# A two-layer decoder trunk in split fp32: low parts of the weights made by ScalarE and accumulating transfers instead of subtractions

## The chip, the cores and the metric

The kernel runs on one core of a Trainium2 chip. A core has five engines with queues of their own: TensorE (PE in the rows; its weight loads are PEld), VectorE (DVE), ScalarE (ACT), GpSimd (POOL) and SyncE (SP, which here only issues loads and stores), and 16 DMA engines that all queues share. The metric is the device time of one execution in microseconds; lower is better.

## The reference, cut to what matters

```python
h = jnp.concatenate([meta, x], axis=1)                     # 16 + 512 tokens, 1024 channels
for i in range(2):
    if i == 0:
        h = h + fox_conformer_mixer(rms_norm(h, ...), w_in, ..., w_out)
    else:
        h = h + multiscale_pool_mixer(rms_norm(h, ...), pool_w, pool_b, pool_scale)
    h = h + conv_glu_ffn(rms_norm(h, ...), w_up[i], conv_w[i], conv_b[i], w_down[i])
return rms_norm(h, final_norm)[:, 16:]

def fox_conformer_mixer(h, ...):
    q, k, v, f_logit, glu = split(h @ w_in)                # 8 heads of 64, 2 x 512 gated channels
    attn = softmax attention over q, k, v with forgetting (cumulated log sigmoid of f_logit)
    u = silu(layer_norm(causal_depthwise_conv(a * sigmoid(g), width 31)))
    return concatenate([attn, u]) @ w_out
def conv_glu_ffn(h, ...):
    u = causal_depthwise_conv(h @ w_up, width 3)           # 2 x 2816 channels
    gate, val = split(u); return (silu(gate) * val) @ w_down
```

All is computed in float32. The pooling mixer takes means over the last 2, 4, 8 or 16 tokens, less the token itself, and multiplies by one 256 x 256 matrix for each quarter of the channels.

## The kernel before

Channels lie on the partitions, the 528 tokens on the free axis. A float32 product is made from rounded parts: each activation x is split as xH + xL and each weight w as wH + wL, and of the four products xH wH, xL wH and xH wL are summed in PSUM (`product`, line 199; every matmul is issued by `mm`, line 197, and carries that line). A weight tile is 128 x 128; with two halves of 264 tokens it takes 6 matmuls.

The 1296 weight tiles come in the order in which TensorE uses them, as 162 chunks of 8 tiles (128 x 1024 float32, 512 KB each): 0 to 27 the mixer, 28 to 93 the first MLP, 94 and 95 the pooling, 96 to 161 the second MLP. `prepare(c)` (line 170) loads one raw chunk through SyncE's queue (line 173), makes wH by a rounding copy on ScalarE (line 223) or, for the 20 chunks of `VECTOR_CHUNKS`, on VectorE (line 224), and makes wL = raw - wH by a subtraction (line 178) on GpSimd for the 29 chunks of `POOL_CHUNKS`, else on VectorE. raw, wH and wL come from a pool of three buffers each; once the MLPs have begun, every fourth chunk takes its tiles from a further pool, `more`, which makes four. `ahead` (line 181) has two chunks prepared beyond the one in use.

Other places that are spoken of: `done_a` and `done_g` (lines 464 and 471) scale the gated projections, line 494 is a tap of the width-31 convolution on VectorE and line 498 one on GpSimd; lines 463 to 720 are the attention, with maxima (659, 663) and low parts of the probabilities (717). `scaled` (line 256) makes xH on ScalarE (258) and xL on VectorE (259). In the pooling, lines 1009 to 1036 scale by the norm, take window sums and add the residual. MLP tiles leave PSUM at line 952 and pass the width-3 convolution at 919 and 922. The norm's chain is line 277 to 283.

The framework orders each engine's instructions by a simulated time. Exceptions are blocks in which an order is written out by hand: the mixer (TensorE), the pooling (TensorE and VectorE) and the end (TensorE). Each engine's queue is served in order.

Of the kernel before, what the change touches and what calls it, by code (L numbers as in the profile page):

```python
# [15 lines left out]
P = 128  # L16
# [36 lines left out]
# output projection in two passes: (tile of the output, tiles of the contraction)  # L53
OUT_ORDER = [(m, (0, 1, 2)) for m in range(8)] + [(m, (4, 5, 6, 7, 3)) for m in range(8)]
# first tile of the output projection whose halves take PSUM from both pools
OUT_WIDE = 3
OUT_JOINT = 1
# tiles of the convolution branch split by VectorE alone
SPLIT_V = (0, 3)
POOL_CHUNKS = (6, 7, 8, 10, 13, 14, 15, 16, 17, 18, 19, 20, 21, 22, 23, 24, 25, 28, 31, 34, 97, 98, 100, 101, 102, 104, 105, 106, 107)  # L60
# what the tensor engine does after the gated tiles. F: half a tile of an input projection, O: of the
# output projection; steps of the attention by pair of heads; a stroke: the next entry of PACE.
# [4 lines left out]
# first tiles of an up projection that go through the contraction side by side; tiles that leave PSUM  # L67
# before the norm is known
OUTER = (0, 4)
RAW = (7, 7)  # L70
# last tiles of the output, done by halves of the tokens; their stores: first and last tile, whether GpSimd
# computes them, whether ScalarE's queue takes them
HALVED = (6, 7)
OUT_PARTS = (((0, 4, 1, 0), (4, 8, 0, 1)), ((0, 1, 0, 0), (1, 3, 0, 1), (6, 8, 1, 0), (3, 6, 0, 1)))
# loads at the start: the input tile behind which the gate's weights are split, behind which the first
# weights come, the weights in front of which the table comes, tiles split by VectorE alone
START = (0, 0, 2, (1, 5))
# tiles of the pooling whose residual sum goes to GpSimd
POOL_RES = (1, 2, 3, 4, 5, 7)
POOL_Z = (1, 4, 6)  # L80
# tiles that the norm scales by halves as it comes
# [3 lines left out]
# steps of the pooling by tile: scale by the norm, window, its first tokens, residual, the next product  # L85
POOL_ORDER = ("Z0 Z1 S0 T1 D0 S1 Z2 T0 Z3 X0 S3 S2 D1 T2 T3 D2 X1 D3 Q0 Z4 Z5 S4 S5 X2 T4 T5 D4 Z6 X3 D5 Z7 "
              "S6 X4 Q2 Q5 Q1 S7 T7 T6 X5 D6 D7 X6 Q4 Q3 Q6 X7 Q7")
# taps of the convolution begun behind half a tile of a projection, on VectorE and on ScalarE with GpSimd
PACE = ((0.75, 0.25), (3.75, 5.0), (2.5, 4.5), (5.25, 1.25), (4.0, 1.0), (3.25, 3.0))
# squares of the last tiles that go to the norm by themselves: before the mixer, the MLPs and the pooling  # L90
# [4 lines left out]
# engines of the copies for a pair of heads: q twice, k twice, v (A: ScalarE, V: VectorE, P: GpSimd)  # L95
COPIES = ('AAAAA', 'VAAAV', 'APAAA', 'PAPAV')
# weight chunks whose high part VectorE takes
VECTOR_CHUNKS = (2, 3, 6, 9, 10, 14, 26, 27, 29, 30, 31, 33, 34, 96, 100, 101, 102, 105, 106, 107)
# products of constants that raise the tensor engine's clock while the first loads run
WARM = 12  # L100
# taps of the last tile of channels that go to GpSimd
# [3 lines left out]
def weight_order():  # L105
    """Order in which the tensor engine takes the 128x128 weight tiles."""
    order = []
    for s, i in GLU_ORDER + QKV_ORDER:
        order += [("in", s, i, k) for k in range(KT)]
    for m, ks in OUT_ORDER:  # L110
        order += [("out", k, m) for k in ks]
    for l in range(2):
        if l == 1:
            for g in range(4):
                for m in range(2):
                    order += [("pool", g, k, m) for k in range(2)]
        for half in range(2):
            tiles = [(half * NGH + j, s) for j in range(NGH) for s in range(2)]
            n = OUTER[l] if half == 0 else 0
            order += [("up", l, s, j, k) for k in range(KT) for j, s in tiles[:n]]  # L120
            order += [("up", l, s, j, k) for j, s in tiles[n:] for k in range(KT)]
            for m in range(KT):
                order += [("down", l, half * NGH + j, m) for j in range(NGH)]
    return order
# [3 lines left out]
def trunk_kernel(  # L128
# [39 lines left out]
    prepared = {}  # L168

    def prepare(c):  # L170
        stg = state["more"] if "more" in state and c % 4 == 3 else stg3
        raw = stg.tile([P, CHUNK, P], F32, tag="raw", name=f"raw{c}")
        nc.sync.dma_start(raw, wts[c])
        wH = stg.tile([P, CHUNK, P], F32R, tag="wH", name=f"wH{c}")
        wL = stg.tile([P, CHUNK, P], F32R, tag="wL", name=f"wL{c}")
        copy("V" if c in VECTOR_CHUNKS else "A", wH, raw)
        eng = nc.gpsimd if c in POOL_CHUNKS else nc.vector
        eng.tensor_tensor(wL, raw, wH.bitcast(F32), op=ALU.subtract)  # L178
        prepared[c] = (wH, wL)

    def ahead():
        n = 2
        c = state["pos"] // CHUNK
        while state["emitted"] < min(c + n + 1, NCHK):
            prepare(state["emitted"])
            state["emitted"] += 1
# [12 lines left out]
    def product(ps, wants, act, t0, n, first=True, final=True):  # L199
        """ps[:, half, :n] = sum over the wanted weight tiles of weight.T @ act."""  # L200
# [25 lines left out]
    def after(late, early):  # L226
        """Issue late behind early on their engine."""
# [4 lines left out]
    def use_log_exp(early):  # L232
        """The table set with both Ln and Exp, loaded behind the instruction early."""
# [5 lines left out]
    def squares(m, apart, t0=0, t1=T, part=True):  # L239
        """Adds the squares of h[m] to the running sum, split at its end; the last ones stay apart."""  # L240
# [15 lines left out]
    def scaled(m, gcol, t0=0):  # L256
        """xH + xL = h[m] * g, split exactly."""
# [10 lines left out]
    def rsqrt(out, srcs, scale, bias, follow=None):  # L268
        """out = (scale * src + bias) ** -0.5: exp(-ln/2) and a Newton step. srcs: pieces in PSUM;
        follow(out, columns) comes behind each."""  # L270
# [24 lines left out]
    def inv_rms(pss, t0, early=(), follow=None):  # L295
        """R[:, token] = 1/sqrt(mean square + eps) in every partition."""
# [5 lines left out]
    # ================= layer 0: attention and convolution =================  # L302
    with ExitStack() as mx:
# [12 lines left out]
        # the gate's weights: high parts in columns 0:8, low parts from column 32 on  # L316
        # (in the memory of the attention's values, which come later)
# [24 lines left out]
        # causal masks, side by side as the blocks of the scores lie in PSUM (128 columns, 16 zeros, 128):  # L342
        # upper triangles for the maxima, lower ones for keys on partitions
# [5 lines left out]
        # the residual is read again after the mixer: until then its tiles serve as scratch  # L349
# [7 lines left out]
        # tokens on partitions: values of two heads with ones (high parts) or zeros (low) between  # L357
        # the last 16 tokens: high, high and low parts of the values below each other against high, low
        # and high parts of the weights
# [5 lines left out]
        # stacked operands of the scores. Even heads: rows 0:64 | 64:128  # L365
        #   q1 = high | low   k1 = high | high   q2 = high | decay rows   k2 = low | decay rows
        # odd heads have the two row halves exchanged.
# [53 lines left out]
        def mtile(name, wants, acts, done, alloc=(pp, pp), split_last=False):  # L421
            """Two units, one for each half of the tokens; done(half, psum) follows each."""
            ws = []
            def joint():
                """Both halves, the last weights behind the others of both."""
# [82 lines left out]
        def first_products():  # L508
            """The gates' logits and the first tile, as their operands come in."""
# [20 lines left out]
        def gate_sums():  # L530
# [6 lines left out]
            # log1p(e) = ln(1+e) + (e - ((1+e) - 1)) / (1+e)  # L537
# [62 lines left out]
        def attention(p):  # L600
            """The steps of a pair of heads by name."""
# [22 lines left out]
            # Maxima, queries on partitions. The query's own decay is the same for all its keys: it  # L624
            # stands in a row's scores and in their maximum alike, and their difference is free of it.
            def maxima(hh):
                tl = st[hh]
                N = tl["N"]
                for x, parts in enumerate((((2, 0, 272), (1, 0, 144), (0, 0, 16)), ((3, 0, 400),),
# [10 lines left out]
                    # short products in front of those whose weights load fast  # L640
# [3 lines left out]
                    # the masks cover the last columns of every block  # L644
# [32 lines left out]
            # Scores, keys on partitions; blocks of 128 keys against their causal queries.  # L677
# [3 lines left out]
            def scores(hh):  # L681
                tl = st[hh]
                for x, parts in enumerate(BL):
# [10 lines left out]
                    # short products in front of those whose weights load fast  # L694
# [26 lines left out]
            def combine(hh, g0, g1):  # L721
# [10 lines left out]
                # 1 / sum = exp(-ln(sum))  # L732
# [127 lines left out]
    # the first pool lies where the input projection's PSUM was: its tile is free early  # L860
# [15 lines left out]
    # ================= gated MLP =================  # L876
    SPAN = ((0, TH), (12, 258))

    def up_side(l, tiles):
        """Products of the up projection for a group of tiles, one step of the contraction at a time."""  # L880
# [106 lines left out]
    # ================= layer 1: causal pooling =================  # L987
    # The windows run over tokens and the products over channels: the products come first.
    with ExitStack() as px:
# [24 lines left out]
        def window(m):  # L1014
            w = 2 << m // 2
            sums[m] = s_ = pl.tile([P, T], F32, tag="ws", name=f"ws{m}", bufs=4)
            if w == 2:
                # (a + b) / 2 - b = a / 2 - b / 2; nothing remains of the first token
# [19 lines left out]
        def follow(m):  # L1038
            scaled(m, C_GF + KT)
            step(m)  # L1040
# [14 lines left out]
    # ================= last tiles by halves, final norm =================  # L1055
# [60 lines left out]
def _tiles(v):  # L1116
    """Vector of n*128 features as [128, n]."""
    return v.reshape(-1, P).T
# [76 lines left out]
```

## Time and profile before

| | |
|---|---|
| median of 3 runs (lowest to highest) | 1113.77 us (1112.04 to 1114.65) |
| span of the profiled execution, first to last instruction | 1111.1 us |
| TensorE busy, matmuls | 1044.2 us, 94% of the span |
| VectorE busy | 767.9 us, 69% |
| ScalarE busy | 467.4 us, 42% |
| GpSimd busy | 250.3 us, 23% |
| line 178, subtractions on VectorE | 133, 164.0 us, 1233 ns each |
| line 178, subtractions on GpSimd | 29, 75.3 us, 2598 ns each |

Busy times count neither waiting nor the issuing of transfers. The mean over the span mixes stretches of different kinds: start and norm to 30 us, mixer to about 300, first MLP to about 660, pooling to about 745, second MLP to about 1080, and the last tiles with the final norm. A view by stretch shows which engine has no idle time in each; a view of waits shows on what TensorE's idle time ended.

### The profile page before, as it was taken

To read this page: it belongs to the slowest core of one execution; us is meant where nothing else is said; L and a number is where in the kernel's file an instruction comes from. 1 tells how busy PE (TensorE), PEld (TensorE's weight loads), DVE (VectorE), ACT (ScalarE), POOL (GpSimd) and SP (SyncE) were. 2 spreads that over 40 slices of the span, in tenths; PEclk is the share of its full clock that TensorE was granted. 3 is DMA by queue.
4 is the path that set the end of the run, shared out by engine and by line. 5 is a ranking of instruction groups with operands and counts; after the bars stand their busy time and mean duration, and the time that the engine had idled before them with its cause. 6 is when DMAs were issued, how large, how long until landed. Compare 5 with 4: busy or idle time off the path is not lost. (4 is left out here: it accounts for less than half of the span.)

```text
span 1111.1 us, 19833 instructions
## 1 busy us (share of the span) xinstructions
PE 1044.2 (94%) x8356; PEld 1031.0 (93%) x8356; DVE 767.9 (69%) x1001; ACT 467.4 (42%) x710; POOL 250.3 (23%) x264
## 2 busy tenths in 40 slices
PE   8978699799999999999999999679999999999996
PEld 7877589799999999999999999579999999999995
DVE  7899999997727985236767546957985336767523
ACT  6435465465325553124434435333553124344422
POOL 7656766342500000000000013662000000000012
PEclk8988889999999999999999999899999999999998
DMA  6211111132332222332322222122322222222202
GB/s 222 68 56 57 39 39 40 58 98 75 104 108 96 87 87 94 96 95 79 95 95 89 84 96 77 38 77 77 112 88 91 91 96 95 96 96 81 92 20 76
DMA packets 28665, 93.21 MB, mean 84 GB/s; under 512 B 3616, under 2 KB 5664, under 8 KB 28576
## 3 DMA queue, kind: packets, MB, share of 16 engines
q1 hardware_dynamic: 26720, 90.68, 24.9%
q8 instruction: 66, 1.08, 0.4%
q10 hardware_dynamic: 1344, 1.23, 0.3%
q0 software_dynamic: 512, 0.03, 0.1%
q14 instruction: 23, 0.19, 0.0%
HBM read 89.80 MB, written 2.10 MB: 83 GB/s over the span
## 5 line engine op out<-in xcount | busy, mean ns | idle before, releaser
L197 PE MATMUL up<-xL,wH 128*128 128x264 f32 (+1 forms) x1408 | 287.9, 286 | 14.7 <-DVE xL L259 14.7
L197 PE MATMUL up<-xH,wH 128*128 128x264 f32 (+1 forms) x1408 | 286.5, 285 | 1.1 <-ACT xH L258 1.1
L197 PE MATMUL up<-xH,wL 128*128 128x264 f32 (+1 forms) x1408 | 287.4, 286 | 0.0
L223 ACT CAST wH<-raw 128x1024 fp32r<-128x1024 f32 x142 | 149.0, 1049 | 235.9 <-PE dn L197 120.4
L178 DVE TENSOR_TENSOR wL<-raw,wH 128x1024 fp32r<-128x1024 f32 x133 | 164.0, 1233 | 105.9 <-ACT wH L223 101.8
L197 PEld LDWEIGHTS up<-xL,wH 128*128 128x128 f32 x1408 | 220.4, 191 | 16.0 <-DVE xL L259 16.0
L197 PEld LDWEIGHTS up<-xH,wH 128*128 128x128 f32 x1408 | 220.7, 191 | 1.4 <-ACT xH L258 1.4
L197 PEld LDWEIGHTS up<-xH,wL 128*128 128x128 f32 x1408 | 220.4, 191 | 0.0
L197 PE MATMUL dn<-gH,wL 128*128 128x264 f32 (+1 forms) x704 | 145.4, 283 | 0.0
L197 PE MATMUL dn<-gH,wH 128*128 128x264 f32 (+1 forms) x704 | 145.3, 284 | 0.0
L197 PE MATMUL dn<-gL,wH 128*128 128x264 f32 (+1 forms) x704 | 145.2, 283 | 0.0
L248 POOL TENSOR_TENSOR acc<-acc,sq 128x528 f32<-128x528 f32 (+1 forms) x30 | 45.1, 1504 | 413.1 <-ACT sq L246 412.7
L922 DVE SCALAR_TENSOR_TENSOR t<-u,par,t 128x528 f32<-128x528 f32 (+1 forms) x176 | 132.7, 769 | 2.4 <-ACT t L919 0.4
L197 PEld LDWEIGHTS dn<-gL,wH 128*128 128x128 f32 x704 | 110.2, 189 | 0.1
L197 PEld LDWEIGHTS dn<-gH,wH 128*128 128x128 f32 x704 | 109.9, 188 | 0.1
L197 PEld LDWEIGHTS dn<-gH,wL 128*128 128x128 f32 x704 | 109.7, 188 | 0.0
L952 DVE TENSOR_TENSOR u<-up,R 128x528 f32<-128x528 f32 (+1 forms) x74 | 51.7, 701 | 77.6 <-PE up L197 75.3
L494 DVE SCALAR_TENSOR_TENSOR h<-u,par,h 128x528 f32<-128x528 f32 x88 | 101.1, 1157 | 0.8
L178 POOL TENSOR_TENSOR wL<-raw,wH 128x1024 fp32r<-128x1024 f32 x29 | 75.3, 2598 | 71.3 <-ACT wH L223 30.0
L919 ACT ACTIVATE t<-u,par 128x528 f32<-128x528 f32 (+1 forms) x88 | 71.4, 821 | 10.1 <-DVE gL L215 6.3
L973 DVE TENSOR_TENSOR h<-dn,h 128x528 f32<-128x528 f32 (+1 forms) x30 | 21.0, 700 | 65.4 <-PE dn L197 65.4
L944 POOL MEMSET u<- 128x2 f32 x44 | 4.0, 101 | 263.1 <-DVE t L922 260.8
(248 smaller groups left out, 1646.2 us busy)
## 6 DMA issues: line engine op xcount, KB each, us to landing
raw<-wts SPq DMA_DIRECT2D x162, 512.0 KB, 3.4
h<-hT SPq DMA_DIRECT2D x8, 264.0 KB, 5.6
hm<-hT SPq DMA_DIRECT2D x8, 264.0 KB, 4.7
outT<-y ACTq DMA_DIRECT2D x1, 512.0 KB, 3.1
outT<-y SPq DMA_DIRECT2D x1, 512.0 KB, 3.9
par<-par SPq DMA_DIRECT2D x1, 476.5 KB, 6.5
outT<-y ACTq DMA_DIRECT2D x1, 384.0 KB, 2.8
outT<-y SPq DMA_DIRECT2D x1, 256.0 KB, 2.2
```

Of the source, the lines that this page charges most:

```text
L178: eng.tensor_tensor(wL, raw, wH.bitcast(F32), op=ALU.subtract)
L197: nc.tensor.matmul(out, lhsT, rhs, start=start, stop=stop)
L223: return nc.scalar.copy(out, src)
L248: state["sum"] = nc.gpsimd.tensor_tensor(acc[:, t0:t1], acc[:, t0:t1], sq[:, t0:t1], op=ALU.add)
L494: nc.vector.scalar_tensor_tensor(cv[i], src, cw(i, j), cv[i], op0=ALU.mult, op1=ALU.add)
L919: nc.scalar.activation(t_, uu[:, off + 2:off + 2 + nt], AF.Identity, scale=col(c0 + 2), bias=col(c0 + 3))
L922: nc.vector.scalar_tensor_tensor(t_, uu[:, off + x:off + x + nt], col(c0 + x), t_, op0=ALU.mult, op1=ALU.add)
L944: nc.gpsimd.memset(uu[:, 0:2], 0.0)
L952: nc.vector.tensor_tensor(v2(ud), ps[:, :, :nu], v2(R[:, tu:tu + 2 * nu]), op=ALU.mult)
L973: nc.vector.tensor_tensor(v2(h[m][:, td:]), ps[:, :, :nd], v2(h[m][:, td:]), op=ALU.add)
```

## The change

The copy to wH stays where it was. wL is first written by ScalarE as -wH (line 178 of the changed kernel), and then a transfer issued by GpSimd adds raw to it in place (line 179). This holds for all 162 chunks; `POOL_CHUNKS` is no longer read. No subtraction of weights is left on VectorE or GpSimd, and raw is free again only when the transfer has landed. `ahead` prepares three chunks beyond the one in use once the pool `more` exists. Removed comments apart, this is all; every later line number is higher by one.

```diff
-        eng = nc.gpsimd if c in POOL_CHUNKS else nc.vector
-        eng.tensor_tensor(wL, raw, wH.bitcast(F32), op=ALU.subtract)
+        nc.scalar.mul(wL, wH.bitcast(F32), -1.0)
+        nc.gpsimd.dma_start(wL, raw, accum_op=ALU.add)
...
     def ahead():
-        n = 2
+        n = 3 if "more" in state else 2
```

ScalarE's queue at the start, before: the squares (sq) and the running sum's split (acc_rv) for the norm, copies of the gate's sums (f, flow), and the norm's R; wH is a chunk's high part.

```order
L223 CAST wH_145<-raw_143 128x1024
L246 ACTIVATE sq_176<-h_70 128x528
L868 ACTIVATE pw<-par 128x2 x4
L214 CAST acc_rv<-acc 128x528
L246 ACTIVATE sq_178<-h_71 128x528
L526 COPY f<-zf_259 8x264
L527 COPY flow<-zf_259 8x264
L526 COPY f<-zf_260 8x264
L527 COPY flow<-zf_260 8x264
L277 ACTIVATE R<-ssq_352,eps 128x264
L279 ACTIVATE R<-R 128x264
L280 ACTIVATE rv<-ssq_352,eps 128x264
L277 ACTIVATE R<-ssq_353,eps 128x264
```

After, the same place:

```order
L178 ACTIVATE wL_147<-wH_146 128x1024
L247 ACTIVATE sq_179<-h_70 128x528
L527 COPY f<-zf_262 8x264
L528 COPY flow<-zf_262 8x264
L527 COPY f<-zf_263 8x264
L528 COPY flow<-zf_263 8x264
L215 CAST acc_rv<-acc 128x528
L247 ACTIVATE sq_181<-h_71 128x528
L178 ACTIVATE wL_155<-wH_154 128x1024
L278 ACTIVATE R<-ssq_355,eps 128x264
L178 ACTIVATE wL_437<-wH_436 128x1024
L280 ACTIVATE R<-R 128x264
```

Three multiplications (L178) stand among them, two of them around the first R, and the split of the running sum comes behind the four copies instead of ahead of them.

GpSimd's queue in the mixer, before: transfers that place rows of the forget gate in the keys (k), the gated product u, taps of the convolution added to h_65, and subtractions of weights.

```order
L590 DMA k_1_1_228<-fL 1x16x33
L178 TENSOR_TENSOR wL_617<-raw_614,wH_616 128x1024
L478 TENSOR_TENSOR u_235<-u_235,sg_349 128x528
L178 TENSOR_TENSOR wL_677<-raw_674,wH_676 128x1024
L498 TENSOR_TENSOR h_65<-h_65,tap_1_831 128x528
L178 TENSOR_TENSOR wL_740<-raw_737,wH_739 128x1024
L478 TENSOR_TENSOR u_236<-u_236,sg_350 128x528
L498 TENSOR_TENSOR h_65<-h_65,tap_2_899 128x528
L498 TENSOR_TENSOR h_65<-h_65,tap_3_902 128x528
L498 TENSOR_TENSOR h_65<-h_65,tap_4_905 128x528
```

After, the same place:

```order
L591 DMA k_1_1_231<-fL 1x16x33
L179 DMA wL_623<-raw_620 128x1024
L479 TENSOR_TENSOR u_238<-u_238,sg_352 128x528
L179 DMA wL_684<-raw_681 128x1024
L499 TENSOR_TENSOR h_65<-h_65,tap_1_841 128x528
L499 TENSOR_TENSOR h_65<-h_65,tap_2_910 128x528
L499 TENSOR_TENSOR h_65<-h_65,tap_3_913 128x528
L479 TENSOR_TENSOR u_239<-u_239,sg_353 128x528
L179 DMA wL_748<-raw_745 128x1024
L499 TENSOR_TENSOR h_65<-h_65,tap_4_916 128x528
```

The subtractions are gone, and between the same products and taps stand the transfers (L179 DMA), which wait for the multiplication on ScalarE and then only issue.

VectorE's queue at the end of the pooling, in the order written by hand, before: window sums ws, the residual into h_70, the low parts xL for the second MLP, and casts (L224) to wH.

```order
L1034 SCALAR_TENSOR_TENSOR ws_7925<-z_7614,ws_7925 128x528
L1036 TENSOR_TENSOR h_70<-h_70,ws_7925 128x528
L1034 SCALAR_TENSOR_TENSOR ws_7968<-z_7615,ws_7968 128x528
L259 SCALAR_TENSOR_TENSOR xL_86<-h_70,par,xH_78 128x528
L224 CAST wH_8006<-raw_8004 128x1024
L224 CAST wH_8092<-raw_8090 128x1024
L259 SCALAR_TENSOR_TENSOR xL_87<-h_71,par,xH_79 128x528
L178 TENSOR_TENSOR wL_8150<-raw_8147,wH_8149 128x1024
```

After, the same place:

```order
L1035 SCALAR_TENSOR_TENSOR ws_8032<-z_7717,ws_8032 128x528
L1037 TENSOR_TENSOR h_70<-h_70,ws_8032 128x528
L1035 SCALAR_TENSOR_TENSOR ws_8076<-z_7718,ws_8076 128x528
L260 SCALAR_TENSOR_TENSOR xL_86<-h_70,par,xH_78 128x528
L225 CAST wH_8114<-raw_8112 128x1024
L260 SCALAR_TENSOR_TENSOR xL_87<-h_71,par,xH_79 128x528
L216 TENSOR_TENSOR acc_rt<-acc,acc_rv 128x528
```

One cast fewer stands between the last two xL (it comes earlier, behind xL_84), and the subtraction behind xL_87 is gone.

## Rows read from the trace of the kernel before

**Rows 1.** Busy time by stretch: PE, PEld, DVE, ACT, POOL; clock, DMA share, GB/s.

```profile
0.00:30.00 30.00, 24.95 (x149) 23.47 (x150) 23.40 (x30) 16.86 (x33) 22.73 (x49) 0.89 0.60 213
30.00:200.00 170.00, 139.91 (x1033) 134.25 (x1032) 163.10 (x221) 81.97 (x152) 106.49 (x89) 0.91 0.16 51
200.00:300.00 100.00, 94.76 (x755) 91.08 (x756) 87.37 (x156) 55.38 (x115) 41.05 (x36) 0.98 0.26 83
300.00:660.00 360.00, 360.00 (x2952) 360.00 (x2951) 214.23 (x263) 140.03 (x175) 13.01 (x42) 1.00 0.29 92
660.00:745.00 85.00, 69.13 (x514) 67.54 (x513) 64.31 (x59) 34.37 (x54) 44.62 (x34) 0.92 0.19 63
```

**Rows 2.** Chain that ended last: start us, us, engine and line, instructions.

```profile
734.38 2.79 DVE xL L259
...
908.55 126.91 PE up L197 x1056
```

**Rows 3.** Waits of PE from 30 to 200 us: in total, times, longest.

```profile
PE ps_g L197 <- DVE u L464: 8.7, 4, 3.7
...
PE o L197 <- DVE VL L617: 0.9, 1, 0.9
```

**Rows 4.** Waits of PE from 660 to 745 us.

```profile
PE up L197 <- DVE xL L259: 14.7, 6, 4.5
```

**Rows 5.** Busy time of line 178 alone, by stretch: DVE, POOL.

```profile
30.00:200.00 170.00, 6.32 (x5) 29.12 (x11) 0.91 0.16 51
...
660.00:745.00 85.00, 7.33 (x6) 13.92 (x5) 0.92 0.19 63
```

**Rows 6.** Timeline of DVE: start us, us, line, operation, shapes, number.

```profile
43.39 0.75 DVE L494 SCALAR_TENSOR_TENSOR h<-u,par,h 128x528 f32<-128x528 f32 x1
...
51.30 5.23 DVE L494 SCALAR_TENSOR_TENSOR h<-u,par,h 128x528 f32<-128x528 f32 x3
...
59.41 2.37 DVE L494 SCALAR_TENSOR_TENSOR h<-u,par,h 128x528 f32<-128x528 f32 x3
```

**Rows 7.** Timeline of POOL in the same stretch.

```profile
43.43 2.71 POOL L589 DMA_DIRECT2D k<-fH  x4 [2.74 <-ACT fH L214]
...
51.97 2.37 POOL L178 TENSOR_TENSOR wL<-raw,wH 128x1024 fp32r<-128x1024 f32 x1
```

**Rows 8.** Groups of DVE by form, 30 to 200 us: busy, mean ns, idle.

```profile
L494 DVE SCALAR_TENSOR_TENSOR h<-u,par,h 128x528 f32<-128x528 f32 x75 | 90.7, 1219 | 0.7
```

**Rows 9.** Timelines of the pooling: five rows of DVE, then one of POOL.

```profile
693.38 2.71 DVE L1036 TENSOR_TENSOR h<-h,ws 128x528 f32<-128x528 f32 x1
...
712.63 0.74 DVE L259 SCALAR_TENSOR_TENSOR xL<-h,par,xH 128x528 fp32r<-128x528 f32 x1
713.29 1.21 DVE L178 TENSOR_TENSOR wL<-raw,wH 128x1024 fp32r<-128x1024 f32 x1
...
724.13 2.25 DVE L1029 TENSOR_TENSOR ws<-ws,par 128x16 f32<-128x16 f32 x2
...
728.76 0.71 DVE L1036 TENSOR_TENSOR h<-h,ws 128x528 f32<-128x528 f32 x1
...
692.67 2.85 POOL L178 TENSOR_TENSOR wL<-raw,wH 128x1024 fp32r<-128x1024 f32 x1
```

**Rows 10.** Costliest groups of the page: busy, mean ns, idle before.

```profile
L223 ACT CAST wH<-raw 128x1024 fp32r<-128x1024 f32 x142 | 149.0, 1049 | 235.9 <-PE dn L197 120.4
```

**Rows 11.** Timeline of ACT at the start, with idle time and what ended it.

```profile
25.15 0.48 ACT L277 ACTIVATE R<-ssq,eps 128x264 f32<-128x264 f32 x1 [1.94 <-PE ssq L197]
```

**Rows 12.** DMA, 42 to 50 us: queue share; issues with us to landing.

```profile
q0 software_dynamic: 256, 0.02, 3.8%
...
k<-fH POOLq DMA_DIRECT2D x4, 2.1 KB, 1.7
```

**Rows 13.** Timelines of POOL and PE: low part of chunk 25, its first product.

```profile
269.37 2.39 POOL L178 TENSOR_TENSOR wL<-raw,wH 128x1024 fp32r<-128x1024 f32 x1 [4.14 <-ACT wH L223]
...
278.14 0.29 PE L197 MATMUL wo<-cH,wL 128*128 128x264 f32 x1
```


## The prediction

> **What bounds the kernel now.** I read the stretches first, because the average busy share mixes very different stages [rows 1]. From 300 to 660 us (first MLP) the TensorE column is as long as the stretch, 360.00 of 360, at a granted clock of 1.00; VectorE is busy 214 of 360 there, ScalarE 140. The second MLP (745 to 1080) looks the same: its chain of waits is almost nothing but products [rows 2]. In the MLPs nothing but the products counts, and 1056 of them take 126.91 us, 120.2 ns each; a chunk of 8 weight tiles has 48, so it is used up in 5.77 us. That is the pace at which weights must be prepared.
>
> The other three stretches have holes. From 30 to 200 us TensorE is busy 139.91 of 170 while VectorE is busy 163.10, so VectorE is the bound. The waits of TensorE there say it too [rows 3]: eight groups from 8.7 down to 0.9 us, all on VectorE, 30.1 us in sum. In the pooling (660 to 745) TensorE waits 14.7 us for the low part xL that VectorE makes [rows 4], and the chain that ended last begins with that very xL [rows 2]. At the start (0 to 30) the loads and the norm rule.
>
> So low parts of weights cost time only where VectorE is late: in the mixer and in the pooling.
>
> **What the change takes away.** In 30 to 200 us line 178 takes VectorE 6.32 us (5 subtractions) and GpSimd 29.12 (11); in the pooling 7.33 (6) and 13.92 (5) [rows 5]. The subtractions on GpSimd cost VectorE as well. Three convolution taps of line 494 take 2.37 us together where GpSimd is idle, but 5.23 beside a GpSimd subtraction of 2.37 [rows 6, 7], so 2.9 us are lost to one of those; over the stretch a tap means 1219 ns where 790 is its pace alone [rows 8]. I take 2 us, since some fall beside one-operand work: eleven make 22, less one whose neighbour waits anyway, 20. VectorE is thus relieved of 6.3 + 20 = 26 us of 163 in this stretch. Issuing a transfer from GpSimd does not do this: while it issued four from 43.43 to 46.13, the tap at 43.39 took 0.75 us, as undisturbed [rows 6, 7].
>
> How much of 26 reaches TensorE? At most its 30.1 us of waits, and then ScalarE, PSUM or the next norm is late. VectorE's taps also fill time between the steps that TensorE waits for, so part of the relief only makes idle time, and TensorE keeps its serial chains through the attention. ScalarE gets about 16 more operations of 1.05 us here, on 81.97 busy of 170, some of them ahead of steps of the attention. I take 10, between 0 and 26. From 200 to 300 us TensorE is busy 94.76 of 100 [rows 1]; the gain there is inside the 10.
>
> In the pooling VectorE runs without gaps in a hand-written order from 690.81 to 737. On it lie one subtraction (1.21 us at 713.29) and operations stretched by GpSimd's subtractions: the residual sum at 693.38 took 2.71 us beside one of 2.85, where its like took 0.71 at 728.76 [rows 9], 2.0 too many. Two more such places at about 2 each (724.13 [rows 9] and 734.38, the latter 2.79 us against 0.74 for the same operation at 712.63 [rows 2, 9]): 1.2 + 2.0 + 2 + 2 = 7.2. Two casts that stood before the last xL now stand partly earlier on the same engine, which moves no sum. I take 6, between 0 and 8; what is late next is xH from ScalarE, since a multiplication now stands in front of the last one.
>
> **What it adds.** *ScalarE*: 162 multiplications of 128x1024. The nearest row is its own copy of that size, 1049 ns [rows 10]: 1.05 us a chunk. In an MLP chunk of 5.77 us ScalarE is busy 140.03/360 of the time, 2.25 us; with 1.05 it is 3.3, 57%. Cost nothing, hidden under the products; without that cover it would be 132 x 1.05 = 139 us.
>
> *Startup*: by the order, the running sum's split falls behind four copies, and two multiplications stand around the first R. Before, ScalarE had idled for 1.94 us when ssq let it begin R at 25.15 us [rows 11], so nothing of its own delayed the norm. Two multiplications in that chain cost up to 2 x 1.05; the transfers for the first chunks run beside the input loads, at a DMA share of 0.60 [rows 1]. I take +2, between 0 and +4.
>
> *Transfers*: 162 of 512 KB, in place of none. No row shows an accumulating transfer, nor a big one from GpSimd. Two things can hurt, its throughput and its latency.
>
> Throughput: loads hold the 16 DMA engines 0.29 of the time in the MLP [rows 1], 0.29 x 5.77 = 1.67 us a chunk. So 4.1 us a chunk are left. Lower bound for the new transfer: as a load of the same size, 1.67 us. Upper bound: GpSimd's small transfers, eight of 2.1 KB holding 3.8% of 8 us, 0.30 us [rows 12]; 512 KB is 31 times their 16.9 KB, 9.4 us. These were packets of 66 bytes or so (256 packets), the new one has rows of 4 KB as the loads, so I stand near the lower bound, and count twice a load because two operands are read for each one written: 3.3 us. Sum 4.97 of 5.77, 86%: it fits, and costs 0. At the upper bound it wouldn't fit by far (rival A).
>
> The Trainium skill, "Collectives: The Full Stack", section "Why ReduceScatter is half of AllGather", says that a transfer that adds is not slowed by the adding but by its second source read, and gives 1.93 times the copy. By it this transfer would be some 3.2 us as an estimate and the sum would stay; by the row of the small transfers alone it would be 9.4. No row here shows which holds for 4 KB rows inside one core.
>
> Latency: before, the low part is there 1.2 us (VectorE) or 2.4 (GpSimd) after the copy. Now: multiplication 1.05, issue 0.68 (four in 2.71 [rows 7]), landing 1.7 (small one [rows 12]) plus about 3.3 for the bytes, 5.0; together 6.7, so 4.3 to 5.5 later. Is it hidden? For each chunk I took the time between the end of its subtraction and TensorE's first product with it. The shortest is chunk 1 at the start, 6.3 us, and chunk 25 next, whose GpSimd subtraction ends at 271.76 and whose product begins at 278.14 [rows 13]; chunks 24 to 31 lie between 6.4 and 10, the MLP at 14 to 16. So it just fits. The GpSimd queue is in order: a transfer waits behind gated products and taps, and the k rows of the attention behind it. I take +1 for chunks 24 to 29, between 0 and +4.
>
> *Three ahead*: in the MLPs the copies already ran about three chunks before use, held by buffers. 0.
>
> Sum: -10 (mixer) - 6 (pooling) + 2 (start) + 1 (late mixer) + 0 (MLPs) = -13. The profiled span is 1111.1, so 1098; the median of the runs is 1113.77, 2.7 above that span, so **1101**. Own range: all gains small and costs high gives -2, so 1112; gains near their bounds -26, so 1088.
>
> **Rivals.**
> A (slower): *the transfers bind the MLPs.* If one takes over 4.1 us of the 16 engines, every chunk of both MLPs waits for bytes, the products stop being the bound, and no depth of preparation helps. At three times a load, 5.0 + 1.67 = 6.6 us against 5.77, +0.85 x 132 chunks = +112, less the 13: 1213. At 4.5 us a transfer +0.4 x 132 = +53, 1154. For it: 86% is a close fit on my own number, and the only GpSimd row scales to 9.4. Against: those are tiny packets.
>
> B (no change): *the relief does not reach TensorE.* The attention's chain is serial through ScalarE, which is handed what VectorE loses; in the pooling xH, with a multiplication ahead of it, takes the place of xL. Then the gains are 0 to 5 and the start and the late mixer cost 3: 1111 to 1116. For: TensorE's waits end on many different lines, each short. Against: VectorE is 96% busy there.
>
> C (slightly slower): *latency, not throughput.* With three buffers a copy can start only when TensorE leaves the chunk three back, 17.3 us before the chunk's own end: 11.5 before its use. Multiplication, copy and issue take 2.6 to 3, so a landing above some 8.5 us stalls the mixer's last chunks and both ends of the pooling. Three chunks share the excess, so 13 us would cost (13 - 8.5)/3 = 1.5 on each of ten chunks, +15 against gains of 13, and with GpSimd's queue in order some more: 1117. The MLP has a fourth buffer and stays whole.
>
> That the change does not do what it says is likely only for "three ahead", counted 0.
>
> **Chances.** Forecast 0.53, A 0.25, B 0.14, C 0.08. The range must reach from 1088 into A to leave out no more than 0.2: 1088 to 1180, which takes in the milder half of A. The likeliest case alone is 1088 to 1112. A measurement of this kernel tells 0.2% (2.2 us) from no change: faster 0.55 (the forecast, a bit of B), same 0.11, slower 0.34 (A, C, the rest).
>
> **What would show it.** Right: TensorE still 100% busy in both MLPs at 5.77 us a chunk, and no product of line 197 waiting for a transfer; DMA share in the MLPs about 0.86 or less; line 494 near 0.8 us a tap instead of 1.2; waits of TensorE in 30 to 200 near 20; in the pooling, xL waits near 9. Wrong: the share near 1.0 and products waiting for wL (A); the mixer's waits moved from VectorE to ScalarE with the same sum (B); waits for wL in chunks 24 to 31 alone (C). A clock below 1.00 in the MLPs would mean TensorE is left without work there, and would come with A.

## The result, and the profile after

The changed kernel takes 1095.85 us (median of 4 runs, 1095.1 to 1097.83), the kernel before 1113.28 in the runs beside it: ratio 0.985 (95% interval 0.984 to 0.986), 17.4 us less. The forecast was 1101, within 1088 to 1180. The profiled execution spans 1093.5 us, 17.6 less than before. Lines stand one number higher than before, except for the new pair 178 and 179.

Where the time went is read from three marks in TensorE's timeline: the start of the first `up` product (end of the mixer), the start of the last `dn` product of the first layer (end of the first MLP), the end.

| us, profiled execution | start to first up | first MLP | pooling to the end |
|---|---|---|---|
| before | 295.5 | 386.9 | 428.7 |
| after | 278.0 | 388.5 | 427.0 |
| difference | -17.5 | +1.6 | -1.7 |

By stretch, in the columns of [rows 1]:

```profile
30.00:200.00 170.00, 147.82 (x1131) 142.19 (x1131) 158.22 (x244) 104.69 (x186) 95.11 (x107) 0.93 0.49 115
200.00:300.00 100.00, 97.84 (x793) 94.92 (x792) 64.25 (x129) 64.17 (x116) 30.22 (x40) 1.00 0.64 160
300.00:660.00 360.00, 360.00 (x2953) 360.00 (x2952) 147.87 (x203) 203.14 (x241) 62.43 (x104) 1.00 0.79 182
660.00:745.00 85.00, 70.67 (x530) 68.65 (x530) 52.36 (x56) 43.26 (x67) 37.44 (x38) 0.94 0.58 137
```

In the MLP TensorE is as full as before, at a clock of 1.00, with the DMA engines at 0.79 instead of 0.29. In 30 to 200 us TensorE is busy 147.82 us instead of 139.91, and VectorE still 158.22 of 170: it has not become idle, it gets further. TensorE's waits there are these four groups and six smaller ones (us in total, times, longest); all ten sum to 22.0, against 30.1 before [rows 3]:

```profile
PE o L198 <- DVE PL L718: 4.4, 2, 3.0
PE e L198 <- DVE E L664: 4.1, 2, 2.4
PE ps_v L198 <- DVE h L579: 3.3, 1, 3.3
PE ps_g L198 <- DVE u L465: 3.2, 2, 2.3
```

The new work, from the page (busy us, mean ns, idle before):

```profile
L179 POOL DMA_DIRECT2D wL<-raw x162 | 138.1, 852 | 644.5 <-ACT wL L178 609.6
...
L178 ACT ACTIVATE wL<-wH 128x1024 fp32r<-128x1024 f32 x162 | 170.5, 1052 | 40.0 <-DVE wH L225 17.2
```

A multiplication takes 1052 ns, issuing a transfer 852 ns. What the transfers take is read in the first MLP, from 400 to 500 us (queue: packets, MB, share of the 16 engines; issue: KB, median us to landing):

```profile
q0 software_dynamic: 2426, 8.89, 49.2%
q1 hardware_dynamic: 2448, 8.91, 29.5%
...
wL<-raw POOLq DMA_DIRECT2D x18, 512.0 KB, 6.2
```

8.89 MB are 17 transfers of 512 KB in 49.2 us of all engines, 2.9 us each. A load takes 29.5/17 = 1.73. Together 4.6 of 5.77 us.

The taps by form, all 88 of them (before, from the page; after, all within 30 to 200 us, where only 75 lay before [rows 8]): the mean fell from 1157 to 999 ns.

```profile
L494 DVE SCALAR_TENSOR_TENSOR h<-u,par,h 128x528 f32<-128x528 f32 x88 | 101.1, 1157 | 0.8
```

```profile
L495 DVE SCALAR_TENSOR_TENSOR h<-u,par,h 128x528 f32<-128x528 f32 x88 | 86.8, 999 | 0.9
```

### The profile page after: what moved, and what is told of

The parts are those of the page before. It is cut to its first block, busy times and chain, and to the rows that moved or that the text cites. A ratio compares the mean times of both kernels' runs of the same rounds, so it can differ in the third digit from the quotient of the medians.

```text
span 1093.5 us, 20138 instructions
## 1 busy us (share of the span) xinstructions
PE 1037.5 (95%) x8356; PEld 1023.8 (94%) x8356; DVE 586.6 (54%) x868; ACT 622.4 (57%) x872; POOL 306.1 (28%) x397
## 4 chain that ended last, share of the span: by engine, by line
PE 78%; DVE 13%; ACT 3%; issue 2%; DMA 2%; POOL 1%; DVEq 0%; SPq 0%; POOLq 0%; ACTq 0%
PE up L198 44%; PE dn L198 23%; DVE h L495 5%; PE wo L198 3%; PE ps_v L198 1%; PE ps_a L198 1%; PE s L198 1%; PE o L198 1%; DVE xL L260 1%; DVE N L660 1%; DVE ws L1023 1%; DVE PL L718 1%; PE ps_k L198 1%; DMA raw<-wts 1%; DVE ws L1035 1%
## 5 line engine op out<-in xcount | busy, mean ns | idle before, releaser
L179 POOL DMA_DIRECT2D wL<-raw x162 | 138.1, 852 | 644.5 <-ACT wL L178 609.6
L224 ACT CAST wH<-raw 128x1024 fp32r<-128x1024 f32 x142 | 149.0, 1050 | 220.6 <-PE up L198 110.7
L178 ACT ACTIVATE wL<-wH 128x1024 fp32r<-128x1024 f32 x162 | 170.5, 1052 | 40.0 <-DVE wH L225 17.2
L495 DVE SCALAR_TENSOR_TENSOR h<-u,par,h 128x528 f32<-128x528 f32 x88 | 86.8, 999 | 0.9
L249 POOL TENSOR_TENSOR acc<-acc,sq 128x528 f32<-128x528 f32 (+1 forms) x30 | 45.3, 1508 | 34.6 <-ACT sq L247 34.3
L499 POOL TENSOR_TENSOR h<-h,tap 128x528 f32<-128x528 f32 x32 | 49.4, 1543 | 11.1 <-ACT tap L498 9.9
```

The costliest lines, as they stand in the source:

```text
L178: nc.scalar.mul(wL, wH.bitcast(F32), -1.0)
L179: nc.gpsimd.dma_start(wL, raw, accum_op=ALU.add)
L224: return nc.scalar.copy(out, src)
L249: state["sum"] = nc.gpsimd.tensor_tensor(acc[:, t0:t1], acc[:, t0:t1], sq[:, t0:t1], op=ALU.add)
L495: nc.vector.scalar_tensor_tensor(cv[i], src, cw(i, j), cv[i], op0=ALU.mult, op1=ALU.add)
L499: nc.gpsimd.tensor_tensor(cv[i], cv[i], pr, op=ALU.add)
```

## The experiments

Times are medians of four runs (ten for the fourth row; for the tenth, of three, without its longest, 1165.4). The three marks are those of one profiled execution each, in the tenth row of that longest one:

| us | median | ratio to before (95%) | first up | first MLP | rest |
|---|---|---|---|---|---|
| two ahead everywhere | 1093.7 | 0.982 (0.981, 0.984) | 277.1 | 388.5 | 426.1 |
| mixer's chunks only | 1096.1 | 0.984 (0.983, 0.986) | 279.3 | 386.9 | 428.1 |
| GpSimd's 29 chunks only | 1098.3 | 0.987 (0.985, 0.990) | 281.2 | 386.9 | 426.6 |
| VectorE's 133 chunks only | 1115.7 | 1.003 (1.002, 1.004) | 300.0 | 387.0 | 426.6 |
| casts of 14 chunks on ScalarE | 1088.9 | 0.979 (0.977, 0.980) | 276.4 | 386.9 | 422.1 |
| before, all subtractions on VectorE | 1108.0 | 0.996 (0.994, 0.997) | 290.6 | 386.9 | 428.2 |
| GpSimd occupied, writing | 1101.3 | 0.989 (0.987, 0.992) | 282.3 | 390.7 | 427.3 |
| GpSimd occupied, reading | 1129.1 | 1.014 (1.012, 1.017) | 309.7 | 388.8 | 425.7 |
| half of each load again | 1096.9 | 0.985 (0.984, 0.987) | 279.0 | 388.3 | 427.0 |
| each load twice | 1146.9 | 1.034 (1.028, 1.040) | 276.6 | 426.3 | 460.4 |
| two ahead, 14 casts on ScalarE | 1090.6 | 0.980 (0.978, 0.981) | 281.1 | 386.9 | 422.1 |
| two ahead, all casts on ScalarE | 1091.4 | 0.981 (0.980, 0.983) | 279.9 | 386.9 | 422.0 |

**Which chunks carry the gain.** First the third chunk ahead is undone:

```diff
-        n = 3 if "more" in state else 2
+        n = 2
```

> The changed kernel with two chunks ahead everywhere. Theory (the third chunk ahead was there already through the buffers): same time, 1095.9 +- 1.5, TensorE still busy 360 of 360 us in the first MLP. Rival (the longer way of the low parts is only hidden because a third chunk is prepared earlier): products wait for transfers in the MLPs, 1 us or more per fourth chunk, 1110 or above.

1093.7, 2.2 less rather than the same, and 0.7 below the range. 0.9 of it lies ahead of the first up product, where the edit changes nothing, and the combination with other casts below shows no gain from it. The MLPs don't need the third chunk ahead.

Then the new way is kept for a part of the chunks, with the old subtraction for the others (`cond` stands for the three conditions `c < 28`, `c in POOL_CHUNKS`, `c not in POOL_CHUNKS`):

```diff
+        if cond:
             nc.scalar.mul(wL, wH.bitcast(F32), -1.0)
             nc.gpsimd.dma_start(wL, raw, accum_op=ALU.add)
+        else:
+            eng = nc.gpsimd if c in POOL_CHUNKS else nc.vector
+            eng.tensor_tensor(wL, raw, wH.bitcast(F32), op=ALU.subtract)
```

> Multiplication and transfer for chunks 0 to 27 (mixer) alone; all later low parts by the old subtractions on VectorE or GpSimd. Theory (the gain is the mixer's, nothing of it comes from the MLPs): the first up product again near 278 us instead of 295.5, the first MLP without the 1.6 us that the change lost there, the pooling back at its old length (+1.8): 1113.3 - 17.5 = 1095.8, within 2. Rival (the later part of the mixer or the pooling needs the relief that chunks 28 and on give): 1100 or more.

1096.1, as the theory had it: the mixer alone carries the gain, and the 134 later chunks add none and take none (-1.6 in the first MLP, +1.1 in the rest).

> Multiplication and transfer only for the 29 chunks whose low part GpSimd subtracted; the 133 others stay subtractions on VectorE. Theory (GpSimd's subtractions slow VectorE's two-operand work, and that is the larger part): taps of line 495 fall from 101.1 us to 87 in all as in the changed kernel, 14.3 of the 25.5 us taken off VectorE in the mixer, so about 56% of 17.5: the first up product near 286, pooling a little shorter, 1102 (1099 to 1105). Rival (VectorE's own subtractions are what counts): 1108 or more.

1098.3, better than either had it. The 29 chunks that GpSimd subtracted bring 14.3 of the 17.5 us of the mixer, and the taps fall all the way (by form, 30 to 250 us: busy, mean ns, idle):

```profile
L499 DVE SCALAR_TENSOR_TENSOR h<-u,par,h 128x528 f32<-128x528 f32 x88 | 86.7, 991 | 1.0
```

> The other half: multiplication and transfer for the 133 chunks that VectorE subtracted; GpSimd's 29 subtractions stay. Theory: taps stay near 101 us, VectorE loses its 9 subtractions of the mixer (11.2 us), so about 44% of 17.5, less 1 for the wait at the start of the first MLP: 1106 (1103 to 1109). Rival (own subtractions count for most): 1100 or less.

1115.7: a miss in its sign. Taking 9 subtractions off VectorE in the mixer, 11.2 us of its time, gains nothing while GpSimd's stay; the first up product comes 4.5 us later than before. The taps are slow still:

```profile
L499 DVE SCALAR_TENSOR_TENSOR h<-u,par,h 128x528 f32<-128x528 f32 x88 | 95.3, 1094 | 1.0
```

So the two halves don't add up as VectorE's busy time would. The trace shows where the time goes. Until 200 us TensorE gets nearly as far as in the changed kernel (1120 products from 30 us on, against 1131 there and 1033 before). Then it waits once, for the layer norm's sum `mu`, which GpSimd makes behind the last tap on VectorE; from 200 to 250 us the granted clock is 0.80, against 1.00 in the changed kernel (waits of TensorE from 200 to 250 us):

```profile
PE mu L202 <- POOL mu L772: 11.4, 1, 11.4
```

The theory's 44% of 17.5 us would have put the mark at 287.8; the wait is 11.4 of the 12.2 us by which 300.0 misses that. The last tap began at 230.6 us, against 222.4 before and 197.7 in the changed kernel. In VectorE's queue, which the framework sorts anew after each edit of the mixer, it stands behind 201 operations other than taps and weights; behind 180 before, 171 in the changed kernel and 153 in the run with GpSimd's 29 chunks. How much of the lateness is this order, and how much the taps' slowness, no run separates.

**Is it GpSimd's time, or what it reads?** The kernel before, without GpSimd's subtractions and without any new transfer:

```diff
-POOL_CHUNKS = (6, 7, 8, 10, 13, ... , 105, 106, 107)
+POOL_CHUNKS = ()
```

> The kernel before, with the 29 subtractions of GpSimd given to VectorE; no transfer that adds. Theory (GpSimd's subtractions cost VectorE about as much time as it would need for them itself): the taps fall to 87 us, but VectorE takes 18 more subtractions of 1.22 us in the mixer, so the same as the kernel before within 4, 1113 (1109 to 1117). Rival (GpSimd's own queue was late, and relieving it is the gain): near the run with the 29 chunks moved alone, 1098 to 1103.

1108.0, 4.6 less than before and 1 below the range. VectorE has 20 subtractions between 30 and 250 us, and is better off for it:

```profile
L494 DVE SCALAR_TENSOR_TENSOR h<-u,par,h 128x528 f32<-128x528 f32 x88 | 85.0, 983 | 0.6
L178 DVE TENSOR_TENSOR wL<-raw,wH 128x1024 fp32r<-128x1024 f32 x20 | 25.7, 1283 | 2.2 <-ACT wH L223 2.2
```

The taps need 85.0 us, 16 less than the 101.1 of the page before, which pays for most of the 18 subtractions added in the mixer (18 x 1.28 = 23). Where the rest and the gain come from isn't shown: other operations no longer collide either (line 717, 128x272: 434 ns against 665), and VectorE's queue is sorted otherwise (148 operations ahead of the last tap). In this kernel the 29 subtractions cost more on GpSimd than on VectorE itself.

Then GpSimd's time is given back to it in the changed kernel, for the 13 chunks 6, 7, 8, 10 and 13 to 21, once by work that only writes and once by work that reads as the subtraction did (both edits in one, shortened; `occ` is a scratch tile, results are thrown away):

```diff
         nc.gpsimd.dma_start(wL, raw, accum_op=ALU.add)
+        if c in (6, 7, 8, 10, 13, ..., 21):
+            nc.gpsimd.tensor_copy(occ[:, 0:1], wH[:, 0, 0:1])       # writing: a tiny copy,
+            for r in range(8):
+                nc.gpsimd.memset(occ, 0.0)                          # eight memsets of 128x320
...
+            for r in range(4):                                      # reading: the old subtraction,
+                nc.gpsimd.tensor_tensor(occ[:, :256], raw[:, 2 * r:2 * r + 2, :],
+                                        wH[:, 2 * r:2 * r + 2, :], op=ALU.subtract)   # in quarters
```

> The changed kernel, with GpSimd occupied again for 13 chunks of the mixer (6, 7, 8, 10, 13 to 21) by one small copy and eight memsets of 128x320 into a scratch tile, some 2.5 us a chunk, that read almost nothing. Theory (reading beside VectorE is what costs): as the changed kernel, taps near 87 us, the first up product at 278 to 281, 1096 to 1099. Rival (GpSimd's time is what costs): 13 of 18 parts of the gain gone, the first up product near 290, 1108.

> As the run with memsets, but GpSimd's occupation is the old subtraction of raw and wH in four pieces, into the scratch tile, thrown away: it reads two operands. Theory: taps back near 98 us, the first up product near 290, 1106 to 1110. If it comes out as the run with memsets, reading is not the cause, whatever both are.

Writing, GpSimd's group and two groups of VectorE (by form, 40 to 250 and 30 to 250 us):

```profile
L183 POOL MEMSET occ<- 128x320 f32 x104 | 43.3, 416 | 3.8
```

```profile
L500 DVE SCALAR_TENSOR_TENSOR h<-u,par,h 128x528 f32<-128x528 f32 x88 | 89.1, 1024 | 1.0
L723 DVE TENSOR_TENSOR PL<-P,PH 128x272 fp32r<-128x272 f32 x16 | 8.9, 560 | 1.1 <-ACT P L722 1.0
```

Reading, the same three:

```profile
L182 POOL TENSOR_TENSOR occ<-raw,wH 128x256 f32<-128x256 f32 x52 | 53.4, 1026 | 1.4
```

```profile
L500 DVE SCALAR_TENSOR_TENSOR h<-u,par,h 128x528 f32<-128x528 f32 x88 | 95.7, 1099 | 1.2
L723 DVE TENSOR_TENSOR PL<-P,PH 128x272 fp32r<-128x272 f32 x12 | 13.4, 1127 | 0.6 <-ACT P L722 0.6
```

GpSimd is occupied alike, 43.3 us (49.0 with the copies) and 53.4. Writing puts the first up product at 282.3, 4.3 later than in the changed kernel; reading at 309.7, 31.7 later. Low parts of the probabilities (line 723, which TensorE waits for) take 560 ns in the mean of the writing run and 1127 in the reading one. Both runs came out above their ranges (1101.3 and 1129.1). Their difference of 28 us at nearly equal occupation speaks for reading, but isn't all due to it directly. In the reading run TensorE again waits once for `mu`, and the last tap begins at 242.8 us behind 201 operations, against 195.2 behind 161 in the writing run (waits of TensorE, 200 to 250 us):

```profile
PE mu L202 <- POOL mu L773: 13.3, 1, 13.3
```

What decides are the taps one by one, whatever their order. Beside an idle GpSimd they take 0.76 us in the mean, in either run. The 14 that lie beside memsets and nothing else of GpSimd take 0.75 to 0.77. The 16 that lie for more than half their time beside the reading quarters take 1.36 in the mean; in the kernel before, the 11 that lie so beside a subtraction take 2.37. So GpSimd's reading stretches a tap, and its memsets don't. The quarters took 4 x 1.03 = 4.1 us a chunk where the whole subtraction had taken 2.6, so this puts back more than the change took away.

**What the change spoiled.** In two places a cast on VectorE is now in the way (next section). The 14 casts of chunks 26 to 107 go to ScalarE:

```diff
-VECTOR_CHUNKS = (2, 3, 6, 9, 10, 14, 26, 27, 29, 30, 31, 33, 34, 96, 100, ... , 107)
+VECTOR_CHUNKS = (2, 3, 6, 9, 10, 14)
```

> The changed kernel with the 14 casts of chunks 26 to 107 that VectorE makes given to ScalarE. Theory (a cast on VectorE now holds work behind it in two places: in the pooling ScalarE's multiplication waits for VectorE's cast, and the last xH and xL stand behind it, 1.8 us idle on VectorE and 3.1 on ScalarE; at the start of the first MLP a cast waits for a load that starts later, and xL behind it, 1.6 us): pooling to end shorter by 3 to 5, first MLP back to 386.9 us from 388.5, together 1091 (1089 to 1093). Rival (ScalarE's queue takes over as what is late): 1095 or more.

1088.9: 7 us less than the changed kernel, the best of all runs, and a hair below the range. The first MLP is back at 386.9 and the rest shorter by 4.9. In the pooling, though, one half of the expectation is wrong (ScalarE, then VectorE, from the span's start):

```profile
707.45 1.05 ACT L224 CAST wH<-raw 128x1024 fp32r<-128x1024 f32 x1
708.52 1.06 ACT L178 ACTIVATE wL<-wH 128x1024 fp32r<-128x1024 f32 x1
709.49 0.72 ACT L259 ACTIVATE xH<-h,par 128x528 fp32r<-128x528 f32 x1
```

```profile
710.25 2.42 DVE L260 SCALAR_TENSOR_TENSOR xL<-h,par,xH 128x528 fp32r<-128x528 f32 x1 [1.60 <-ACT xH L259]
```

Cast and multiplication still stand in front of the last xH, and VectorE still idles 1.60 us for it, against 1.80. What went are VectorE's own casts in that chain, 0.68 + 1.80 + 1.81 = 4.3 us.

**How far the transfers were from binding.** In the MLPs part of each raw chunk is loaded a second time, to the same place with the same values:

```diff
         nc.sync.dma_start(raw, wts[c])
+        if 35 <= c < 94 or c >= 108:
+            nc.sync.dma_start(raw[:, :4, :], wts[c][:, :4, :])      # half; in the other run all of it
```

> The changed kernel, with half of each raw chunk loaded a second time in the MLPs (chunks 35 to 93 and 108 to 161; the values stay as they are). It asks how far the transfers were from binding: the 16 DMA engines are at 0.79 of the time there, 49.2% for the adding transfers (2.9 us each) and 29.5% for the loads. Theory (what binds is the sum of the transfers' time against 5.77 us a chunk): 0.79 + 0.15 = 0.94, still hidden, as the changed kernel, 1096 (1094 to 1099). Rival (queueing binds well before the sum reaches 1): products wait for low parts, DMA share below 0.9, 1105 or more.

> As before, with the whole raw chunk loaded twice in the MLPs. Theory: 0.79 + 0.29 = 1.08 of the time, so a chunk takes 1.08 x 5.77 = 6.23 us, 0.46 more for each of 113 chunks: +52, 1148 (1135 to 1165), DMA share near 1, TensorE waiting for transfers. Rival (loads and adding transfers overlap better than their busy time says): 1110 or less.

From 330 to 630 us, first with half, then with all loaded again, in the columns of [rows 1], and TensorE's largest wait of the second (us in total, times, longest):

```profile
330.00:630.00 300.00, 300.00 (x2459) 300.00 (x2459) 133.96 (x187) 171.60 (x200) 49.40 (x91) 1.00 0.91 224
```

```profile
330.00:630.00 300.00, 279.93 (x2239) 276.73 (x2238) 119.33 (x170) 149.93 (x175) 41.89 (x82) 0.99 0.90 241
```

```profile
PE up L200 <- DMA wL<-raw: 16.2, 10, 3.0
```

At a DMA share of 0.91 TensorE is still full; with the whole load twice it waits for the low parts' transfers, and the time is 1146.9, where the sum gave 1148. The runs of that one scatter from 1146 to 1165 and the profiled one is the longest, so its kind of wait is read here, not its size. The share there is 0.90 and not near 1 as expected: the transfers begin to bind between these two runs, somewhat before the 16 engines are busy all the time. That the sum of their time against 5.77 us sets the point is borne out to that extent, and not shown more closely.

**Together.** Two ahead and fewer casts on VectorE:

> Two chunks ahead instead of three, and the 14 casts of chunks 26 to 107 on ScalarE: what the runs so far favour, together. If both hold: 1088.9 less what two ahead gave (2.2, of which 1.1 lay at the start, where the code is the same): 1087.8 (1086 to 1089.5). If two ahead was only scatter: 1088.9.

> As the run before, and the six casts of the mixer's early chunks (2, 3, 6, 9, 10, 14) on ScalarE too. VectorE, the bound from 30 to 200 us, loses 4 casts of 0.7 to 1 us there; ScalarE, at 105 of 170 us, gains 4 of 1.05 and stands in the norm's chain at the start. Theory (VectorE's time is worth about 0.7 of itself): 2 to 3 less, 1085.5. Rival (ScalarE is on the chain at the start): 1088 or more.

1090.6 is above its range; 1091.4 is where the rival had it (1088 or more). The MLPs and the rest are as in the run with 14 casts (386.9 and 422). The difference between that run and the first of these lies ahead of the first up product, 276.4 against 281.1 us, where both kernels hold the same instructions in the same order: one execution's mixer can differ by that much from another's. Two microseconds between medians of four are therefore taken as no finding here, the 2.2 of two ahead among them, marks of the mixer are good to some microseconds only, and giving the six early casts to ScalarE gains nothing that shows.

## Why the prediction was right

**What bounds, and what goes away.** Right: the MLPs hid everything, and the time came from the mixer. The contention read off three rows (a tap of 790 ns stretched beside GpSimd's subtraction, [rows 6, 7]) is borne out tap by tap, and taking away GpSimd's subtractions alone brought most of the gain. What share of the 17.5 us belongs to the new order of VectorE's queue isn't separated; ahead of the last tap it differs little between the two kernels (180 operations and 171).

The Trainium skill, "SBUF — State Buffer", section "Who interferes with whom", says that a VectorE instruction with two SBUF inputs contends with a GpSimd instruction that reads SBUF, not with one that only writes. The taps agree: 0.75 to 0.77 us beside nothing but memsets, 1.36 in the mean beside reading.

**The mixer: -10 forecast, -17.5 measured.** The relief of VectorE was sized well, 26 us against 14.3 (taps) + 11.2 (nine subtractions) = 25.5, though it was made up otherwise: the taps lost 14.3 and not 20, and four more subtractions lay between 200 and 300 us. The step that failed is the share of it that reaches TensorE: less than half was taken, it was 0.7. Nor is VectorE's busy time the right coin: taking 11 us of own subtractions off it gained nothing, with TensorE waiting for 11.4 us behind one late tap, and giving it 18 more in place of GpSimd's gained 4.6. A collision also stretches the short operations that TensorE waits for (line 723 above). Of the prediction's signs, the waits came true (22.0 us, near 20), but a tap takes 1.0 us in the mean and not 0.8: GpSimd's own taps and products stay, and 23 taps that lie for more than half their time beside a two-operand instruction of GpSimd still take 1.64.

**Pooling: -6 forecast, -1.7 measured.** The terms one by one, in the timelines after (VectorE, ScalarE, GpSimd; start us, us):

```profile
678.00 1.65 DVE L1037 TENSOR_TENSOR h<-h,ws 128x528 f32<-128x528 f32 x1
...
704.19 1.80 DVE L225 CAST wH<-raw 128x1024 fp32r<-128x1024 f32 x1
...
707.19 0.26 DVE L1030 TENSOR_TENSOR ws<-ws,par 128x16 f32<-128x16 f32 x2
...
713.46 1.81 DVE L225 CAST wH<-raw 128x1024 fp32r<-128x1024 f32 x1
717.06 2.40 DVE L260 SCALAR_TENSOR_TENSOR xL<-h,par,xH 128x528 fp32r<-128x528 f32 x1 [1.80 <-ACT xH L259]
```

```profile
715.35 1.06 ACT L178 ACTIVATE wL<-wH 128x1024 fp32r<-128x1024 f32 x1 [3.08 <-issue]
716.31 0.72 ACT L259 ACTIVATE xH<-h,par 128x528 fp32r<-128x528 f32 x1
```

```profile
717.31 3.33 POOL L249 TENSOR_TENSOR acc<-acc,sq 128x528 f32<-128x528 f32 x2
```

The subtraction is gone (-1.21 [rows 9]). The residual sum fell only from 2.71 to 1.65, the pair of short products from 2.25 to 0.26 as forecast, the last xL only from 2.8 [rows 2] to 2.4: GpSimd's sums of squares (717.31) read beside it now instead of subtractions. Together -4.7. Against it stand casts that take 4.3 us instead of 3.1, two of them stretched to 1.8, and a wait of 1.80 us that is new: the multiplication at 715.35 stands in ScalarE's queue in front of the last xH and needs the high part that VectorE casts until 715.27. So -4.7 + 1.2 + 1.8 = -1.7, the measured difference, but that it fits to the tenth is partly luck: three more operations changed (a window sum -1.1, an xL -1.0, another window sum +1.5), and the norm ahead took 0.5 longer. TensorE's waits for xL fell to 12.4 us only, where about 9 was the sign. The prediction had named the multiplication in front of xH as late next, and priced it at nothing; it did not see that its input comes from VectorE.

**Startup: +2 forecast, about 0 measured.** Two multiplications do lie around the first R, as the order said (ScalarE):

```profile
25.18 0.48 ACT L278 ACTIVATE R<-ssq,eps 128x264 f32<-128x264 f32 x1 [0.62 <-PE ssq L198]
25.56 1.05 ACT L178 ACTIVATE wL<-wH 128x1024 fp32r<-128x1024 f32 x1
26.50 0.41 ACT L280 ACTIVATE R<-R 128x264 f32<-128x264 f32 x1
```

R began at 25.18 us, against 25.15 before [rows 11], and the exponential came 0.84 later (26.50 against 25.66). But TensorE had the first ps_g product at 25.92, against 25.89: the first products didn't wait for R. The third waited 0.30 us for its low part's transfer, and by 30 us TensorE had begun 144 products, against 149 before.

**Late mixer: +1 forecast, +1.6 measured, elsewhere.** In the mixer's last chunks no low part was late; the one wait of any size for a transfer, 1.6 us for ps_a in the waits from 30 to 200 us, came at 34.6 us. But at the start of the first MLP a cast on VectorE waits for a load that starts with the last product of the output projection (before too). That load took 6.51 us beside the adding transfers (278.25 to 284.76 in the chain of waits), where 4.5 had passed from issue to cast before; and the last xL, ahead of that cast in the old order (298.02 and 300.19), now stands behind it:

```profile
284.88 0.69 DVE L225 CAST wH<-raw 128x1024 fp32r<-128x1024 f32 x1 [4.63 <-DMA raw<-wts]
285.50 0.76 DVE L260 SCALAR_TENSOR_TENSOR xL<-h,par,xH 128x528 fp32r<-128x528 f32 x1
```

TensorE waited 1.1 us for that xL. With the cast on ScalarE the 1.6 us are gone.

**Rivals.** A did not come, and the experiment on loads shows why and how near it was: 4.6 of 5.77 us, with 0.91 of the engines' time still hidden. An adding transfer took 2.9 us where the forecast took 3.3, so the guess of twice a load (1.73) was 0.4 high per transfer; the bound from GpSimd's small transfers (9.4) was far off for rows of 4 KB. In A's own sum three times a load makes 5.0 + 1.67 = 6.7 us, not 6.6, so +0.90 x 132 = +119 and 1220 instead of 1213. B came in part, in the pooling alone. C did not: landing took 5.8 us in the median (5.0 forecast), under the 8.5 from which it would have cost.

The Trainium skill, "Collectives: The Full Stack", section "Why ReduceScatter is half of AllGather", gives 1.93 as the measured ratio between a ring's copying and its adding transfers. Here it is 2.9/1.73 = 1.7, an adding transfer within SBUF against a load from HBM; no run has a plain copy within SBUF. The direction agrees, the factor is smaller.

## What to carry to other kernels

Look for GpSimd work that reads SBUF beside a VectorE that is the bound: the price isn't on GpSimd's row but in the stretched means of VectorE's instructions, two-operand ones above all, and even moving that work onto VectorE can pay. Where a tool sorts the queues, look after each edit at where the last operation of a side branch has come to stand: TensorE waited for 11.4 us behind one late tap. A transfer that adds can take such work off both engines if its time and the loads' together leave room in the stretch that TensorE fills. Once a step goes to another engine, look again at every older step that shares a queue with its consumer: 14 casts left on VectorE cost 6.5 us in the first MLP and the rest.

## What the runs showed of the hardware that was not expected

A small transfer issued by GpSimd lands later when adding transfers of 512 KB share its queue: 4.5 us for 2.1 KB, against 1.6 before, and once the issue itself waited 2.7 us, by the profile for one of them (issues, and GpSimd's timeline):

```profile
k<-fH POOLq DMA_DIRECT2D x8, 2.1 KB, 4.5
```

```profile
50.45 0.48 POOL L591 DMA_DIRECT2D k<-fL  x1 [2.70 <-DMA wL<-raw]
```

An adding transfer from one tile of SBUF to another held the 16 DMA engines for 2.9 us per 512 KB, 1.7 times as long as a load of that size, and in the MLPs, up to a share of 0.91, no matmul waited for one.

A cast on VectorE, which reads one operand, is stretched beside GpSimd's reading too: the two of 1.8 us above took place beside sums of squares on GpSimd, where 14 casts beside an idle GpSimd take 0.69 in the mean.
